# Two-layer decoder kernel: the first two products of three stages run tile by tile together

## The chip, the cores and the metric

The kernel runs on one core of a Trainium2 chip, as one program. The metric is device time in microseconds (us). TensorE (PE in the rows) does the matrix products, VectorE (DVE), ScalarE (ACT) and GpSimd (POOL) work elementwise, and all loads named here are issued from the queue of SyncE (SP). Each engine works through its own list of instructions in order and waits at semaphores for the others.

## The reference

Two layers run one after the other on 512 tokens of 1024 features. Each layer normalises its input, projects it into a mixer, adds the output product, normalises again and adds a feed-forward part.

```python
def rms_norm(x, g):
    y = xf * lax.rsqrt(jnp.mean(xf * xf, axis=-1, keepdims=True) + EPS)
    return (y * g.astype(jnp.float32)).astype(x.dtype)
...
def swiglu_ffn(h, w_gate_up, w_down):
    g, u = jnp.split(h @ w_gate_up, 2, axis=-1)
    return (jax.nn.silu(g) * u) @ w_down
...
def hybrid_layer(x, mem, positions, layer_idx, ...):
    proj = rms_norm(x, norm_mix) @ w_in
    mix, qm = dsa_mixer(proj, pos) if layer_idx % 2 == 0 else dilated_mixer(proj, pos)
    mo = memory_attention(qm, mem, norm_mem, w_mem_kv)
    x = x + jnp.concatenate([mix, mo], axis=-1) @ w_out
    return x + swiglu_ffn(rms_norm(x, norm_ffn), w_gate_up, w_down)
```

Layer 1 uses the dilated mixer: three groups of heads with strides 1, 4 and 16, each with query, key and value products and rotary angles. In both layers four more heads attend to 256 memory tokens. A last norm ends the program.

## The kernel before

Activations lie transposed in SBUF: a tile has 128 features by 512 tokens, and `xT` holds eight of them (k = 0 to 7). A product of full precision is made of three fp32r matmuls for each k: the operand is split into a high half (`xh`, `wh`) and a low half (`xl`, `wl`), and `proj` (line 228) adds `wh·xh`, `wh·xl` and `wl·xh` (lines 247 to 249) over eight tiles in one PSUM bank, so a product is 24 matmuls of 512 columns. `proj_steps` (lines 235 to 237) is the same product cut into four steps for interleaving.

A weight chunk is loaded by `load` (line 176) into one of two `wf` buffers; `wsplit` casts it to `wh` on ScalarE (line 48) and subtracts for `wl` on VectorE or GpSimd (line 51). There are three buffers each of `wh` and `wl`.

The norm is applied late. `prep` scales each tile of x by the gain into `xh` (ScalarE, line 331) and `xl` (VectorE, line 332) and sums the squares (ScalarE line 306, GpSimd line 316, VectorE line 275). `ssq_cols` turns the sum into one value per token: eight small matmuls (line 278; four in the program's order) and a chain of twelve small VectorE instructions (lines 256 to 265). `row` spreads these values into a row R: four VectorE instructions (line 288), one product with ones (line 290) and a ScalarE copy (line 293). Finished products are multiplied by R.

Three stages begin in this way; below they are called the entries. The first is `ffn(0)`, the second `layer1`, the third `ffn(1)`. At each, the last output product of the stage before still adds to `xT` tile by tile (`add_x`, line 653) while `prep` follows it, and TensorE starts the first product on the tiles as they come.

In `ffn` each step f makes two products, gate and up, from one `wf` buffer, and a gated activation (lines 676 to 679). In `layer1` the first two products are the memory heads' queries (`qm`). Then `tables` loads the angle tables from DRAM (`saved`) and multiplies them by R on GpSimd, cosine first and sine second (line 411); `memory_back` reloads the memory heads' keys and values (`kept`, line 558). Two generators are then woven: `products` (query, key and value products, `rope` on lines 376 to 384) and `attention`, which starts with `memory_attention`: scores (line 452), their maxima (line 581), exponentials (line 585), transposes (line 469) and the product with the values (line 423).

TensorE's order is the order of the code. The order on the other engines and on SyncE is set by a scheduler that simulates a timeline when the program is built. PSUM has eight banks: two named acc, three S, two T and one O; `psum_any` goes round them.

Of the kernel before, what the change touches and what calls it, by code (L numbers as in the profile page):

```python
# [19 lines left out]
NT = S // 128  # L20
MEM = 256
DFF = 2816
FT = DFF // 128
# [41 lines left out]
class _Trunk:  # L65
# [589 lines left out]
    def ffn(self, l):  # L655
        nc = self.nc
        xh, xl, parts = self.prep(2 if l == 0 else 5)
        src = self.io[f"gu{l}"]
        mh, ml = [], []
        bigs = []  # L660
        for f in range(FT):
            w = self.load(src[f], [2, 1024])
            ps = []
            for j in range(2):
                p = self.psum_any()
                self.proj(p, self.wsplit(w[:, j], nc.gpsimd if j else nc.vector), xh, xl)
                ps.append(p)
                if f == 0:
                    if j == 0:
                        cols = self.ssq_cols(parts)  # L670
                    else:
                        R = self.row(cols, NT)
            g = self.tmp("raw")
            u = self.tmp("raw")
            m = self.tmp("o")
            nc.vector.tensor_tensor(out=g, in0=ps[0], in1=R, op=ALU.mult)
            nc.scalar.activation(g, g, AF.Silu)
            nc.vector.tensor_tensor(out=u, in0=ps[1], in1=R, op=ALU.mult)  # L678
            nc.vector.tensor_tensor(out=m, in0=g, in1=u, op=ALU.mult)
            if f < 12:  # L680
                if f % 4 == 0:
                    bigs = [self.big("midh"), self.big("midl")]
                b = slice((f % 4) * 512, (f % 4 + 1) * 512)
                h, lo = bigs[0][:, b], bigs[1][:, b]
            else:
                h, lo = self.slot("mh"), self.slot("ml")
            _split2(nc, h, lo, m, nc.vector)
            mh.append(h)
            ml.append(lo)
        src = self.io[f"dn{l}"]  # L690
        for t in range(KT - 1 if l else KT):
            p = self.psum_any()
            for w, k0, k1 in self.down_weights(src[t]):
                self.down(p, w, k0, k1, mh, ml)
            self.add_x(t, p)
        if l:
            self.final(list(self.down_weights(src[KT - 1])), mh, ml)
# [264 lines left out]
    def layer1(self):  # L962
        nc, mm = self.nc, self.nc.tensor.matmul
        xh, xl, parts = self.prep(3)
        ws = self.chunks("in1", list(range(14)), lo=("gpsimd", "vector"), hi=(None, None))
        pq = []
        for j in range(2):
            p = self.psum_any()
            self.proj(p, next(ws), xh, xl)
            pq.append(p)  # L970
            if j == 0:
                cols = self.ssq_cols(parts)
            else:
                R = self.row(cols, NT)
                self.cols4 = self.ssq_cols(parts, by_residue=True)
        cs, sn = self.tables(R, 0)
        qm = [self.plain(p, R, 0.125, "qm") for p in pq]
        self.memory_back()
# [4 lines left out]
        qk0, QK = [[], []], [[[], []], [[], []]]  # L983
# [3 lines left out]
            while what not in done:  # L987
                yield

        def qk(g, dst):  # L990
            p = self.psum("acc")
            yield from self.proj_steps(p, next(ws), xh, xl)
            dst.append(self.rope(p, cs, sn, self.slot("qkh"), self.slot("qkl"), by_residue=g > 0))

        def g0_scores(pr, i):
# [111 lines left out]

        def products():
            yield from qk(0, qk0[0])
            yield from qk(0, qk0[0])  # L1110
            yield from qk(0, qk0[1])
            done.add("qk0")
            yield from qk(0, qk0[1])
            yield from values(0)
            done.add("qk1")
            done.add("v0")
            for g in range(2):
                for _ in range(2):
                    yield from qk(1, QK[0][g])
            for n, _ in enumerate(values(1)):  # L1120
                if n == 4:
                    done.add("qk2")
                yield
            yield from qk(1, QK[1][0])
            yield from qk(1, QK[1][0])
            yield from until("o0")
            yield from qk(1, QK[1][1])
            yield from qk(1, QK[1][1])
            for n, _ in enumerate(values(2)):
                if n == 0:  # L1130
                    mem_out = [(o, self.inverse(den)) for o, den in self.mem_out]
                if n == 4:
                    done.add("qk3")
                if n == 4:
                    mem_out = [self.finish_pair(*a) for a in mem_out]
                yield
            done.add("v12")
            out = self.out_proj("out1a", mem_out)
            yield from itertools.islice(out, 4)
            yield from until("all")  # L1140
            yield from out

        def attention():
# [43 lines left out]
            yield from finish(1)  # L1187
            done.add("all")

        first, second = products(), attention()  # L1190
        _weave(itertools.islice(first, 24), itertools.islice(second, 12), na=2)
        _weave(first, second)
        for _ in self.out_proj("out1b", outs):
            pass
# [182 lines left out]
```

## Time and profile before

| | |
|---|---|
| median of three runs | 1252.84 us |
| lowest and highest | 1252.38 and 1262.76 us |
| profiled execution, own time | 1258.64 us |
| its span, first to last instruction | 1256.9 us |
| mean granted TensorE clock in the span | 0.984 |

The rows used below come from the profiled execution, whose times count from the start of its span. Matmuls are pipelined, so a matmul of 512 columns is shown with 0.39 us though the next starts about 0.23 us after it. [...]

### The profile page before, as it was taken

The page shows a single profiled execution, that of the slowest core. Times are in us where ns is not written, and L with a number is a line of the kernel's source. Part 1 is how long each engine was busy: PE and PEld are TensorE (multiplying, and loading weights), DVE is VectorE, ACT ScalarE, POOL GpSimd, SP SyncE. Part 2 cuts the span into 40 slices and gives each one's busy share as a digit, 9 for nine tenths or more (in the row PEclk, how much of TensorE's full clock was granted, in tenths as well). Part 3 has the DMA queues.
Part 4 walks back from the last instruction along what each step waited for, and adds up shares of the span by engine and source line. Part 5 has one row for each costly group of instructions (what it writes and reads, how often), then busy time and mean ns, then how long its engine had stood idle before and what let it go on. Part 6 is the DMA issues. An engine that isn't in the chain of part 4 may idle for free.

```text
span 1256.9 us, 14343 instructions
## 1 busy us (share of the span) xinstructions
PE 1209.4 (96%) x5624; PEld 952.3 (76%) x5624; DVE 530.6 (42%) x1024; ACT 484.8 (39%) x852; POOL 345.6 (27%) x218
## 2 busy tenths in 40 slices
PE   9799899999999999999998999999999999999997
PEld 5368566576888888888887778887788888888886
DVE  4759823548333323322224544449433333332112
ACT  3663675424332322322222666545323222322222
POOL 0424553244212222122222223324222222211222
PEclk9889999999999999999999999999899999999999
DMA  5312212202122222222223110221122222222221
GB/s 194 123 34 101 83 37 83 69 34 101 67 101 101 101 87 82 101 64 110 107 106 116 68 68 34 67 68 67 68 101 101 98 79 92 101 93 92 92 93 67
DMA packets 29185, 108.36 MB, mean 86 GB/s; under 512 B 2494, under 2 KB 11582, under 8 KB 20670
## 3 DMA queue, kind: packets, MB, share of 16 engines
q1 hardware_dynamic: 28574, 106.93, 24.1%
q8 instruction: 44, 0.72, 0.2%
q10 hardware_dynamic: 544, 0.52, 0.1%
q14 instruction: 23, 0.19, 0.0%
HBM read 104.43 MB, written 3.01 MB: 85 GB/s over the span
## 4 chain that ended last, share of the span: by engine, by line
PE 78%; DVE 10%; DMA 4%; ACT 3%; issue 3%; POOL 1%; SPq 0%; DVEq 0%; ACTq 0%; POOLq 0%
PE psS L248 5%; PE psS L247 5%; PE psS L249 5%; PE psT L247 3%; PE psT L248 3%; PE psT L249 3%; PE psacc L247 3%; PE psacc L248 3%; PE psacc L249 3%; PE psacc L222 3%; PE psS L222 3%; PE psS L224 3%; PE psS L223 3%; PE psacc L224 3%; PE psacc L223 3%
## 5 line engine op out<-in xcount | busy, mean ns | idle before, releaser
L51 POOL TENSOR_TENSOR wl<-wf,wh 128x1024 fp32r<-128x1024 f32 x90 | 216.9, 2411 | 643.6 <-ACT wh L48 590.5
L48 ACT CAST wh<-wf 128x1024 fp32r<-128x1024 f32 (+1 forms) x163 | 167.6, 1029 | 516.5 <-issue 166.1
L51 DVE TENSOR_TENSOR wl<-wf,wh 128x1024 fp32r<-128x1024 f32 x86 | 104.0, 1210 | 88.6 <-ACT wh L48 88.6
L248 PE MATMUL psS<-xl,wh 128*128 128x512 f32 x272 | 107.7, 396 | 2.8 <-DVE xl L332 2.8
L247 PE MATMUL psS<-xh,wh 128*128 128x512 f32 x272 | 108.2, 398 | 0.0
L249 PE MATMUL psS<-xh,wl 128*128 128x512 f32 x272 | 106.9, 393 | 0.0
L247 PE MATMUL psacc<-xh,wh 128*128 128x512 f32 x192 | 76.9, 401 | 0.0
L248 PE MATMUL psacc<-xl,wh 128*128 128x512 f32 x192 | 76.9, 401 | 0.0
L249 PE MATMUL psacc<-xh,wl 128*128 128x512 f32 x192 | 76.4, 398 | 0.0
L247 PE MATMUL psT<-xh,wh 128*128 128x512 f32 x184 | 73.4, 399 | 0.0
L248 PE MATMUL psT<-xl,wh 128*128 128x512 f32 x184 | 73.3, 398 | 0.0
L249 PE MATMUL psT<-xh,wl 128*128 128x512 f32 x184 | 72.8, 396 | 0.0
L316 POOL TENSOR_TENSOR ssq<-ssq,t 128x512 f32<-128x512 f32 (+1 forms) x31 | 42.4, 1367 | 96.2 <-ACT t L306 61.0
L248 PEld LDWEIGHTS psS<-xl,wh 128*128 128x128 f32 x272 | 51.3, 188 | 14.8 <-DVE xl L332 3.3
L235 PE MATMUL psacc<-xh,wh 128*128 128x512 f32 x144 | 61.6, 428 | 0.0
L247 PEld LDWEIGHTS psS<-xh,wh 128*128 128x128 f32 x272 | 51.2, 188 | 12.3 <-issue 0.5
L249 PEld LDWEIGHTS psS<-xh,wl 128*128 128x128 f32 x272 | 51.2, 188 | 11.7
L678 DVE TENSOR_TENSOR raw<-psacc,R 128x512 f32<-128x512 f32 x22 | 15.2, 691 | 102.0 <-PE psacc L249 102.0
L237 PE MATMUL psacc<-xh,wl 128*128 128x512 f32 x144 | 56.9, 395 | 0.0
L236 PE MATMUL psacc<-xl,wh 128*128 128x512 f32 x144 | 56.8, 395 | 0.0
L653 DVE TENSOR_TENSOR xT<-xT,psacc 128x512 f32<-128x512 f32 x44 | 30.0, 683 | 39.0 <-PE psacc L224 38.8
L379 ACT COPY raw<-psacc 32x512 f32<-32x512 f32 x72 | 41.6, 578 | 6.1 <-DVE raw L376 5.1
(320 smaller groups left out, 2634.6 us busy)
## 6 DMA issues: line engine op xcount, KB each, us to landing
wf<-in_gu SPq DMA_DIRECT2D x44, 1024.0 KB
wf<-in_dn SPq DMA_DIRECT2D x16, 1024.0 KB
wf<-in_in SPq DMA_DIRECT2D x12, 1024.0 KB
wf<-in_dn SPq DMA_DIRECT2D x16, 384.0 KB
wf<-in_v SPq DMA_DIRECT2D x3, 1024.0 KB
wf<-in_in SPq DMA_DIRECT2D x5, 512.0 KB
xT<-in_x SPq DMA_DIRECT2D x8, 256.0 KB
wf<-in_mk SPq DMA_DIRECT2D x2, 1024.0 KB
```

What stands on the lines that cost most here:

```text
L48: nc.scalar.copy(hi, src)
L51: lo_engine.tensor_tensor(out=lo, in0=src, in1=hi.bitcast(F32), op=ALU.subtract)
L222: mm(out, wh[k], xh[k], start=first and k == 0, stop=False)
L223: mm(out, wh[k], xl[k], start=False, stop=False)
L224: mm(out, wl[k], xh[k], start=False, stop=last and k == n - 1)
L235: mm(out, wh[:, s], xh[k], start=k == 0, stop=False)
L236: mm(out, wh[:, s], xl[k], start=False, stop=False)
L237: mm(out, wl[:, s], xh[k], start=False, stop=k == KT - 1)
L247: mm(out, wh[:, s], xh[k], start=k == 0, stop=False)
L248: mm(out, wh[:, s], xl[k], start=False, stop=False)
L249: mm(out, wl[:, s], xh[k], start=False, stop=k == KT - 1)
L316: engine.tensor_tensor(out=parts[part], in0=parts[part], in1=sq, op=ALU.add)
```

## The change

In both feed-forward parts and in layer 1 the first two products now run together: for each tile k the three matmuls of the one and then those of the other. Their sum of squares goes to TensorE after both, one more product follows, and only then the row R. In `ffn` the gated activation of step 0 therefore comes within step 1, and the low half of step 1's gate weights moves from VectorE to GpSimd. In layer 1 the third product is the first query product of group 0, made before the row in a T bank instead of an acc bank; its rope and two further steps of `products` come ahead of the weave with the memory attention.

```diff
--- before.py
+++ after.py
@@ -658,18 +658,8 @@
         src = self.io[f"gu{l}"]
         mh, ml = [], []
         bigs = []
-        for f in range(FT):
-            w = self.load(src[f], [2, 1024])
-            ps = []
-            for j in range(2):
-                p = self.psum_any()
-                self.proj(p, self.wsplit(w[:, j], nc.gpsimd if j else nc.vector), xh, xl)
-                ps.append(p)
-                if f == 0:
-                    if j == 0:
-                        cols = self.ssq_cols(parts)
-                    else:
-                        R = self.row(cols, NT)
+
+        def swiglu(f, ps):
             g = self.tmp("raw")
             u = self.tmp("raw")
             m = self.tmp("o")
@@ -679,7 +669,7 @@
             nc.vector.tensor_tensor(out=m, in0=g, in1=u, op=ALU.mult)
             if f < 12:
                 if f % 4 == 0:
-                    bigs = [self.big("midh"), self.big("midl")]
+                    bigs[:] = [self.big("midh"), self.big("midl")]
                 b = slice((f % 4) * 512, (f % 4 + 1) * 512)
                 h, lo = bigs[0][:, b], bigs[1][:, b]
             else:
@@ -687,6 +677,22 @@
             _split2(nc, h, lo, m, nc.vector)
             mh.append(h)
             ml.append(lo)
+
+        for f in range(FT):
+            w = self.load(src[f], [2, 1024])
+            ps = [self.psum_any() for _ in range(2)]
+            ws = [self.wsplit(w[:, j], nc.gpsimd if j or f == 1 else nc.vector) for j in range(2)]
+            if f == 0:
+                self.projs(list(zip(ps, ws)), xh, xl)
+                cols = self.ssq_cols(parts)
+                first = ps
+                continue
+            for j in range(2):
+                self.proj(ps[j], ws[j], xh, xl)
+                if f == 1 and j == 0:
+                    R = self.row(cols, NT)
+                    swiglu(0, first)
+            swiglu(f, ps)
         src = self.io[f"dn{l}"]
         for t in range(KT - 1 if l else KT):
             p = self.psum_any()
@@ -963,16 +969,13 @@
         nc, mm = self.nc, self.nc.tensor.matmul
         xh, xl, parts = self.prep(3)
         ws = self.chunks("in1", list(range(14)), lo=("gpsimd", "vector"), hi=(None, None))
-        pq = []
-        for j in range(2):
-            p = self.psum_any()
-            self.proj(p, next(ws), xh, xl)
-            pq.append(p)
-            if j == 0:
-                cols = self.ssq_cols(parts)
-            else:
-                R = self.row(cols, NT)
-                self.cols4 = self.ssq_cols(parts, by_residue=True)
+        pq = [self.psum_any() for _ in range(2)]
+        self.projs([(p, next(ws)) for p in pq], xh, xl)
+        cols = self.ssq_cols(parts)
+        p = self.psum("T")
+        self.proj(p, next(ws), xh, xl)
+        R = self.row(cols, NT)
+        self.cols4 = self.ssq_cols(parts, by_residue=True)
         cs, sn = self.tables(R, 0)
         qm = [self.plain(p, R, 0.125, "qm") for p in pq]
         self.memory_back()
@@ -987,9 +990,10 @@
             while what not in done:
                 yield
 
-        def qk(g, dst):
-            p = self.psum("acc")
-            yield from self.proj_steps(p, next(ws), xh, xl)
+        def qk(g, dst, p=None):
+            if p is None:
+                p = self.psum("acc")
+                yield from self.proj_steps(p, next(ws), xh, xl)
             dst.append(self.rope(p, cs, sn, self.slot("qkh"), self.slot("qkl"), by_residue=g > 0))
 
         def g0_scores(pr, i):
@@ -1106,7 +1110,6 @@
             outs.append((hi, lo))
 
         def products():
-            yield from qk(0, qk0[0])
             yield from qk(0, qk0[0])
             yield from qk(0, qk0[1])
             done.add("qk0")
@@ -1187,8 +1190,12 @@
             yield from finish(1)
             done.add("all")
 
+        for _ in qk(0, qk0[0], p):
+            pass
         first, second = products(), attention()
-        _weave(itertools.islice(first, 24), itertools.islice(second, 12), na=2)
+        for _ in itertools.islice(first, 2):
+            pass
+        _weave(itertools.islice(first, 20), itertools.islice(second, 12), na=2)
         _weave(first, second)
         for _ in self.out_proj("out1b", outs):
             pass
```

TensorE at the entry of `ffn(0)`, end of the first product and what follows it. In these names the number counts tiles: `psS_2420` is the bank of the gate product, `psT_2471` or `psT_2421` that of the up product, `xl_2398` the second half of the low tiles. Before:

```order
L247 MATMUL psS_2420<-xh_2397,wh_2421 128x512 [waits Activation_49]
L248 MATMUL psS_2420<-xl_2398,wh_2421 128x512 [waits DVE_49]
L249 MATMUL psS_2420<-xh_2397,wl_2422 128x512
L278 MATMUL psacc_2449<-ones_71,ssq_2380 128x2 [waits DVE_49]
L278 MATMUL psacc_2449<-ones_71,ssq_2380 128x2 x3
L247 MATMUL psT_2471<-xh_2376,wh_2472 128x512 [waits PE_49]
L248 MATMUL psT_2471<-xl_2377,wh_2472 128x512
```

After:

```order
L247 MATMUL psS_2420<-xh_2397,wh_2422 128x512 [waits Activation_49]
L248 MATMUL psS_2420<-xl_2398,wh_2422 128x512 [waits DVE_49]
L249 MATMUL psS_2420<-xh_2397,wl_2423 128x512
L247 MATMUL psT_2421<-xh_2397,wh_2426 128x512
L248 MATMUL psT_2421<-xl_2398,wh_2426 128x512
L249 MATMUL psT_2421<-xh_2397,wl_2427 128x512
L278 MATMUL psacc_2478<-ones_71,ssq_2380 128x2 [waits DVE_49]
L278 MATMUL psacc_2478<-ones_71,ssq_2380 128x2 x3
L247 MATMUL psS_2502<-xh_2376,wh_2504 128x512
```

The up product now takes each tile right behind the gate product, and the small matmuls of the squares stand behind both.

VectorE at the same entry: the last low tile, the sum of squares and the begin of the chain for the norm (`rs_v`, `rs_i`, `rs_y`). Before:

```order
L51 TENSOR_TENSOR wl_2524<-wf_2520,wh_2523 128x1024 [waits DMAHW1_49,Activation_49,Pool_49]
L332 SCALAR_TENSOR_TENSOR xl_2398<-xT_79,gains_80,xh_2397 128x512 [waits Activation_49]
L275 TENSOR_TENSOR ssq_2380<-ssq_2380,ssq_2416 128x512 [waits Pool_49]
L256 TENSOR_SCALAR rs_v_2455<-psacc_2449 128x4 [waits PE_49]
L260 TENSOR_SCALAR rs_i_2457<-rs_v_2455 128x4 [waits DVE_49]
L261 TENSOR_SCALAR rs_y_2458<-rs_i_2457 128x4 [waits DVE_49]
L263 TENSOR_TENSOR rs_q_2459<-rs_y_2458 128x4 [waits DVE_49]
```

After:

```order
L332 SCALAR_TENSOR_TENSOR xl_2398<-xT_79,gains_80,xh_2397 128x512 [waits Activation_49] x2
L275 TENSOR_TENSOR ssq_2380<-ssq_2380,ssq_2416 128x512 [waits Pool_49]
L256 TENSOR_SCALAR rs_v_2484<-psacc_2478 128x4 [waits PE_49]
L260 TENSOR_SCALAR rs_i_2486<-rs_v_2484 128x4 [waits DVE_49]
L51 TENSOR_TENSOR wl_2594<-wf_2589,wh_2593 128x1024 [waits DMAHW2_49,Activation_49]
L261 TENSOR_SCALAR rs_y_2487<-rs_i_2486 128x4 [waits DVE_49]
L263 TENSOR_TENSOR rs_q_2488<-rs_y_2487 128x4 [waits DVE_49]
```

The low half of step 1's gate weights (`wl_2524`) has left the place ahead of the last `xl`, and the low half of step 2's gate weights (`wl_2594`) now stands inside the chain of the norm.

VectorE in layer 1, where the memory attention starts (`nm` is the maximum of the scores). Before, from the first maximum on:

```order
L581 TENSOR_REDUCE nm_4870<-psS_4864 128x2 [waits PE_49]
L581 TENSOR_REDUCE nm_4875<-psS_4865 128x2 [waits PE_49]
L51 TENSOR_TENSOR wl_5058<-wf_4988,wh_5057 128x1024 [waits DMAHW0_49,PE_49,Activation_49]
L581 TENSOR_REDUCE nm_4898<-psS_4892 128x2 [waits PE_49]
L581 TENSOR_REDUCE nm_4903<-psS_4893 128x2 [waits PE_49]
L376 TENSOR_TENSOR raw_4910<-psacc_4843,table_4819 128x512 [waits DMAHW2_49,Pool_49]
L498 RECIPROCAL den_4863<-den_4863 128x8 [waits Activation_49]
```

After, up to the second maximum and two rows on:

```order
L50 CAST wh_5093<-wf_5091 128x1024 [waits DMAHW1_49,PE_49]
L384 TENSOR_TENSOR raw_4876<-raw_4876,raw_4877 128x512 [waits Pool_49]
L51 TENSOR_TENSOR wl_5094<-wf_5091,wh_5093 128x1024 [waits DVE_49,PE_49]
L581 TENSOR_REDUCE nm_4924<-psS_4918 128x2 [waits PE_49]
L581 TENSOR_REDUCE nm_4929<-psS_4919 128x2 [waits PE_49]
L51 TENSOR_TENSOR qkl_4875<-raw_4876,qkh_4874 128x512 [waits Activation_49]
L376 TENSOR_TENSOR raw_4936<-psacc_4887,table_4850 128x512 [waits DMAHW2_49]
```

Ahead of the first maximum there now stand the rope's add of the first query product, which waits for GpSimd (`raw_4876`), and the split of the value weights (`wh_5093`, `wl_5094`).

## Rows read from the trace of the kernel before

**Rows 1.** the page, busy time of each engine (share of the span) and instructions.

```profile
PE 1209.4 (96%) x5624; PEld 952.3 (76%) x5624; DVE 530.6 (42%) x1024; ACT 484.8 (39%) x852; POOL 345.6 (27%) x218
```

**Rows 2.** who TensorE waited for: us in total, times, longest.

```profile
PE psS L452 <- DMA kept<-kept: 4.2, 1, 4.2
PE psO L248 <- DVE xl L332: 2.8, 1, 2.8
...
PE psacc L441 <- ACT raw L379: 1.8, 1, 1.8
```

**Rows 3.** windows: stretch, length, busy time by engine, then granted clock, DMA.

```profile
306.60:310.00 3.40, 3.40 (x10) 2.66 (x9) 3.09 (x10) 0.00 (x0) 1.67 (x1) 0.53 0.23 43
691.00:695.50 4.50, 3.89 (x14) 2.79 (x15) 1.29 (x2) 1.56 (x7) 1.27 (x1) 0.62 0.03 11
700.00:740.00 40.00, 38.22 (x238) 30.10 (x236) 18.14 (x27) 26.79 (x58) 10.42 (x7) 1.00 0.15 53
883.00:890.00 7.00, 7.00 (x22) 5.75 (x21) 4.17 (x17) 1.04 (x1) 2.35 (x1) 0.52 0.34 130
```

**Rows 4.** timeline of TensorE, first entry: start, length, instruction, [idle before <- releaser].

```profile
296.18 0.40 PE L247 MATMUL psS<-xh,wh 128*128 128x512 f32 x1
...
304.23 0.50 PE L248 MATMUL psS<-xl,wh 128*128 128x512 f32 x1 [2.84 <-DVE xl L332]
...
304.83 1.05 PE L278 MATMUL psacc<-ones,ssq 128*128 128x2 f32 x8
...
312.92 1.02 PE L290 MATMUL psacc<-raw,ones 128*128 128x512 f32 x2
...
319.38 0.40 PE L247 MATMUL psacc<-xh,wh 128*128 128x512 f32 x1
```

**Rows 5.** timeline of TensorE, third entry, first and seventy-third product matmul.

```profile
874.49 0.39 PE L247 MATMUL psO<-xh,wh 128*128 128x512 f32 x1
...
899.22 0.39 PE L247 MATMUL psT<-xh,wh 128*128 128x512 f32 x1
```

**Rows 6.** timeline of VectorE, first entry.

```profile
300.19 2.32 DVE L51 TENSOR_TENSOR wl<-wf,wh 128x1024 fp32r<-128x1024 f32 x1
302.43 1.75 DVE L332 SCALAR_TENSOR_TENSOR xl<-xT,gains,xh 128x512 fp32r<-128x512 f32 x1
...
306.12 2.17 DVE L260 TENSOR_SCALAR rs_i<-rs_v 128x4 int32<-128x4 int32 x1
...
310.31 0.87 DVE L288 TENSOR_SCALAR raw<-ident,rs_y 128x128 f32<-128x128 f32 x4
```

**Rows 7.** timeline of GpSimd, first entry.

```profile
296.27 7.36 POOL L316 TENSOR_TENSOR ssq<-ssq,t 128x512 f32<-128x512 f32 x4
305.89 2.38 POOL L51 TENSOR_TENSOR wl<-wf,wh 128x1024 fp32r<-128x1024 f32 x1 [2.26 <-PE psacc L278]
```

**Rows 8.** timeline of TensorE, second entry (layer 1).

```profile
669.96 0.40 PE L247 MATMUL psT<-xh,wh 128*128 128x512 f32 x1
...
675.48 0.95 PE L278 MATMUL psacc<-ones,ssq 128*128 128x2 f32 x8
...
684.41 0.48 PE L235 MATMUL psacc<-xh,wh 128*128 128x512 f32 x1
...
691.61 1.63 PE L452 MATMUL psS<-kept,qm 64*128 64x256 f32 x8 [4.20 <-DMA kept<-kept]
```

**Rows 9.** chain of waits in layer 1: start, length, what.

```profile
676.57 1.24 DVE wl L51
...
677.86 0.34 SPq L176
...
679.41 12.07 DMA kept<-kept
```

**Rows 10.** timelines of GpSimd and of VectorE in layer 1.

```profile
691.19 1.27 POOL L411 TENSOR_TENSOR table<-raw,R 128x512 f32<-128x512 f32 x1 [3.56 <-DMA raw<-saved]
...
693.21 1.29 DVE L581 TENSOR_REDUCE nm<-psS 128x2 f32<-128x512 f32 x2 [4.18 <-PE psS L452]
```

## The prediction

> **What bounds the kernel now.** I first read the page's busy times: TensorE is busy 96% of the span [rows 1], so only what shortens TensorE's own list, its waits or its slow stretches can change the time. Then who TensorE waited for: one wait of 4.2 us for `kept` in layer 1, waits of 2.8 us for the low tile `xl`, one of 1.8 us for an acc bank [rows 2]. Then the timeline around each entry: in `ffn(0)` TensorE stands 2.84 us for the last `xl` [rows 4], in `ffn(1)` as long by [rows 2], and in layer 1 it stands 4.20 us ahead of the first memory score [rows 8]. Last, the granted clock by windows, since waits may be followed by slow matmuls. They are: behind these three waits the clock falls to 0.53 for 3.40 us, to 0.52 for 7.00 us and to 0.62 for 4.50 us, while 40 us of ordinary work in layer 1 run at 1.00 [rows 3]. A stretch at granted clock c loses its length times 1 - c: 1.6, 3.3 and 1.7 us, 6.6 in all. So the three entries hold 2.84 + 2.84 + 4.20 = 9.9 us of waiting and 6.6 us of slow clock, 16.5 of 1257.
>
> A cross-check: 24 matmuls from 669.96 to 675.48 give 0.23 us a matmul [rows 8]. Three products are 72 of them, 16.6 us; with the small matmuls of the squares, 1.05, and the row's, 1.02 [rows 4], 18.6. TensorE took 23.2 from 296.18 to 319.38 [rows 4] and 24.7 from 874.49 to 899.22 [rows 5]: 4.6 and 6.1 too many, which is wait plus clock (2.84 + 1.6, 2.84 + 3.3).
>
> **The change, the feed-forward entries.** Nothing is computed less; matmuls, casts and loads are the same in number. What moves is when TensorE wants things.
>
> The last `xl`. Before, VectorE did step 1's `wl`, 2.32 us at 300.19, and then the last `xl`, 1.75 us from 302.43 [rows 6], while TensorE wanted it some 2.84 us sooner than 304.23. After, TensorE comes to the last tile behind 42 matmuls, at 296.18 + 42 x 0.23 = 305.8, later than 304.2 even if `xl` came no sooner, and without that `wl` it comes about 2.3 sooner. This wait goes for certain.
>
> What is late next: the sum of squares. GpSimd now gets step 1's low half between the adds that end at 303.63 before (four, 7.36 us [rows 7], so 1.84 each). It adds one op of 2.38 us [rows 7], so the last add ends at about 306; VectorE's add is taken at 0.65, as a maximum in [rows 10]. TensorE wants it behind 48 matmuls, at 307.2. Covered, with some 0.5 to 1 us to spare; if GpSimd is later than that, each us shows as a wait on the L278 matmuls.
>
> Then the row. It is wanted one product later: 307.2 + 1.05 + 5.5 = 313.8. The chain on VectorE starts at about 308.3. Before, its second instruction took 2.17 us from 306.12 [rows 6], and ended as GpSimd's `wl` of 2.38 us from 305.89 ended [rows 7]. The order has such a `wl` on GpSimd at that place again, so the chain is held till about 310.2. Then `wl_2594` stands in it, 1.24 us as in [rows 9]; the rest of the chain took 310.31 - 308.29 = 2.0 us, and the four writes of the row 0.87 [rows 6]. That is 314.3, 0.5 us behind TensorE; at the ends, the hold may be absent (no wait) or the whole chain 0.4 later (0.8). I take 0.4 of new wait at each entry. The later activation of step 0 lies beside TensorE's products, since the banks go round eight.
>
> [...]
>
> So each `ffn` gains 2.84 - 0.4 = 2.4 us, 4.9 for both.
>
> **The change, layer 1.** Here the wait is for a load, `kept`, which has nothing to do with `xl`. SyncE's queue goes in order. The chain reads: `wl` on VectorE at 676.57, 1.24 us, then an issue on SyncE at 677.86 and then `kept`, 12.07 us from 679.41 [rows 9]: a weight load that waits for a `wf` buffer stands ahead of `saved` and `kept`. That `wl` follows a cast whose buffer is free when TensorE has read the first product's `wh` for the last time: 675.4 before, but 680.4 now, since both products end together (46 instead of 24 matmuls from 669.96, and 5 us are 22 of them). So everything behind it comes 4.9 us later: `kept` is there at 679.41 + 12.07 + 4.9 = 696.4, and the sine table, multiplied from 691.19 [rows 10], starts at 696.1.
>
> TensorE comes to the first score behind two products, 11.0 us, the work that stood from 675.48 to 684.41 [rows 8], 8.9, and one more product of 24 matmuls, 5.5: at 695.4, some 0.3 later with a short wait for the row. So it waits about 0.7 for `kept` instead of 4.20: the added matmuls cover a load that came later, and most of the wait goes.
>
> A new wait follows. By the order, VectorE has a rope add ahead of the first maxima, which needs GpSimd's sine table (1.27 us [rows 10]) and a GpSimd product of the same size: 696.1 + 1.27 + 1.27 = 698.6. The add and a maximum are each taken at 0.65, half of the pair in [rows 10], and the `wl` between them is 1.24 again: the first two maxima end at 701.2, and the exponentials that free a score bank at about 702.4 (as long as the two maxima, 1.29). TensorE comes to the second score at 696.4 + 1.0 + 12 matmuls x 0.23 = about 700.4: 2 us of wait, which wasn't there. Behind it the order shows three more places where a bank is taken over quickly (a T bank, an acc bank, the product with the values); each lies between nothing and the 1.8 us of the acc bank in [rows 2], and I take 0.3, 1 and 1. Sum after: 0.7 + 2 + 0.3 + 1 + 1 = 5.0, against 4.2 + 1.8 = 6.0 before. Layer 1 gains 1 us, with bounds of 3 to either side.
>
> **The clock.** If no entry holds a long wait, the three slow stretches go, 6.6 us. The 1.8 us wait of [rows 2] lies in the 40 us at 1.00 [rows 3], so waits of 0.4 to 2 us should not bring them back. But the profiled execution took 1258.64 us, 5.8 more than the median of 1252.84, and it may be that the runs of the median lose less to the clock than the one traced. I count half, 3.3, with ends of nothing and 6.6.
>
> [...]
>
> **Sum.** Against the profiled execution: feed-forward -4.9, layer 1 -1.0, clock -6.6 in full: 1258.6 - 12.5 = 1246.1. Against the median, with half of the clock: 1252.84 - 4.9 - 1.0 - 3.3 = 1243.6, so 1244.
>
> **Rivals.**
> 1. The clock comes back in full in the median too, and layer 1 does as summed or better: 1252.84 - 12.5 = 1240, to 1237.5 when layer 1 gains 3 us more. For it: each of the three waits is followed by such a stretch, and the rest is at 1.00. Against: the median lies below the trace.
> 2. The gain of layer 1 and of its clock is eaten there: the waits at the scores, the T bank and the acc bank add up to 8 instead of 5, and no clock is gained anywhere. 1252.84 - 4.9 + 2 = 1250; with half of the clock of the feed-forward entries, 2.4, 1247.5. I price it at 1248. For it: VectorE's list has two waits on GpSimd ahead of work that TensorE wants.
> 3. Slower: VectorE stands at the rope add for the sine table, and with it the maxima and all that TensorE wants. Each us that the table is later than 696.1 is a us of TensorE. From 9 us later, 705, the change loses; if the shifted loads land as late again as `kept` takes, 12.07, the time is 1252.84 - 9.2 + 12.1 = 1256. For it: `saved` goes through the queue that the change delays. Against: [rows 9] shows that queue held by one wait only.
> 4. VectorE's chain for the row is held by GpSimd not once but twice, 2.38 us each [rows 7], in both feed-forward entries: the new wait there is 0.4 + 2.4 = 2.8 us, as long as the one removed, and the clock falls behind it as before. Then only layer 1 gains, 1.0 and half of its clock, 0.8: 1251. For it: the 2.17 us in the chain [rows 6] and one more low half on GpSimd. Against: the order puts that one ahead of the chain, not beside it.
>
> That the entries go on waiting for `xl` is excluded by 305.8 against 304.2.
>
> **How the numbers follow.** Forecast 0.43, rival 1 0.30, rival 2 0.17, rivals 3 and 4 0.05 each. About 1%, 12.5 us, is what a measurement of this kernel tells from no change: faster is below 1240.3, slower above 1265.4. Faster by that: two thirds of rival 1, 0.20, and the better quarter or so of the forecast, 0.13. Slower: 0.03, the bad end of rival 3. The range goes from the clock in full with layer 1 three us better, 1252.84 - 15.5 = 1237, to no clock and layer 1 three us worse than summed, 1252.84 - 5.9 + 3 = 1250.
>
> **What the changed profile would show.** Right: no wait of 2 us or more for `xl`; the fourth product's start 18.6 to 19.4 us behind the entry's first matmul; granted clock 1.00 in both feed-forward entries; the row's wait at L290 below 1 us; the weight load ahead of `kept` issued some 5 us later against the entry's start; a wait for `kept` under 1.5 us and a new one of about 2 at the second score. Wrong: a wait at L278 (GpSimd too late), a clock of 0.5 behind a short wait, or VectorE held at the rope add for more than 4 us. I would be wrong by much if the tail of layer 1's memory attention, which I priced by three guesses, opens gaps of more than 2 us each, or if the products made two steps earlier also shorten its end.

## The result and the profile after

The changed kernel took 1241.08 us (1237.89 to 1243.12, 4 runs) against 1252.61 (1248.98 to 1262.76, 4 runs): ratio 0.989, interval 0.984 to 0.994. A second group on another chip gave 0.988, interval 0.985 to 0.991. The forecast was 1244, the range 1237 to 1250, so the time lies inside it, nearer to rival 1 (1240) than to the forecast. The profiled execution has a span of 1236.0 us.

Who TensorE waited for, the lines that answer to [rows 2]: the two waits for `xl` and the one for `kept` are gone; the row costs 0.8 us in three waits, the acc bank 0.8 instead of 1.8. (Of the 2.8 for `raw`, 2.0 lie in layer 0.)

```profile
PE psS L452 <- ACT raw L585: 2.8, 2, 2.0
...
PE psacc L441 <- ACT raw L379: 0.8, 1, 0.8
...
PE psacc L290 <- DVE raw L288: 0.8, 3, 0.3
```

TensorE at the first entry (start, length, instruction, idle time before), beside [rows 4]: the squares follow 48 product matmuls without a wait, the row waits 0.21 us, and the fourth product starts 310.24 - 291.91 = 18.3 us behind the first matmul, where it was 23.2.

```profile
291.91 0.39 PE L247 MATMUL psS<-xh,wh 128*128 128x512 f32 x1
...
302.90 0.95 PE L278 MATMUL psacc<-ones,ssq 128*128 128x2 f32 x8
...
309.68 1.12 PE L290 MATMUL psacc<-raw,ones 128*128 128x512 f32 x2 [0.21 <-DVE raw L288]
310.24 0.79 PE L247 MATMUL psacc<-xh,wh 128*128 128x512 f32 x1
```

The third entry, beside [rows 5]: 877.90 - 858.71 = 19.2 us instead of 24.7, with one new wait of 0.56 us ahead of the second product's first matmul: its bank still held an output product, which VectorE had to add to the residual sum `xT` first.

```profile
858.71 0.40 PE L247 MATMUL psO<-xh,wh 128*128 128x512 f32 x1
...
860.12 0.47 PE L247 MATMUL psacc<-xh,wh 128*128 128x512 f32 x1 [0.56 <-DVE xT L653]
...
877.37 1.10 PE L290 MATMUL psacc<-raw,ones 128*128 128x512 f32 x2 [0.28 <-DVE raw L288]
877.90 0.79 PE L247 MATMUL psT<-xh,wh 128*128 128x512 f32 x1
```

VectorE and GpSimd at the first entry, beside [rows 6, 7]. The last two `xl` end at 298.82, and TensorE came to that tile at about 301.5. The squares are ready at 302.07 and wanted at 302.90: 0.8 us to spare. The chain's second instruction again ends with GpSimd's `wl` (304.08 + 1.65 against 303.31 + 2.40), and `wl` stands inside the chain.

```profile
294.80 4.02 DVE L332 SCALAR_TENSOR_TENSOR xl<-xT,gains,xh 128x512 fp32r<-128x512 f32 x2
301.38 0.69 DVE L275 TENSOR_TENSOR ssq<-ssq 128x512 f32<-128x512 f32 x1 [2.56 <-POOL ssq L316]
...
304.08 1.65 DVE L260 TENSOR_SCALAR rs_i<-rs_v 128x4 int32<-128x4 int32 x1
305.65 1.22 DVE L51 TENSOR_TENSOR wl<-wf,wh 128x1024 fp32r<-128x1024 f32 x1
...
308.75 0.87 DVE L288 TENSOR_SCALAR raw<-ident,rs_y 128x128 f32<-128x128 f32 x4
...
303.31 2.40 POOL L51 TENSOR_TENSOR wl<-wf,wh 128x1024 fp32r<-128x1024 f32 x1 [1.97 <-ACT wh L48]
```

Layer 1, TensorE, then SyncE's queue and GpSimd, beside [rows 8 to 10]. The value weights' load is issued 669.41 - 656.70 = 12.7 us behind the entry's first matmul, where it was 7.9, and `saved` and `kept` behind it; all the same the first score doesn't wait, and the second waits 0.83 us.

```profile
656.70 0.40 PE L247 MATMUL psT<-xh,wh 128*128 128x512 f32 x1
...
674.58 1.13 PE L290 MATMUL psacc<-raw,ones 128*128 128x512 f32 x2 [0.29 <-DVE raw L288]
675.54 1.80 PE L278 MATMUL psacc<-ones,ssq 128*128 128x2 f32 x8
...
684.52 1.13 PE L452 MATMUL psS<-kept,qm 64*128 64x256 f32 x8
...
690.09 1.13 PE L452 MATMUL psS<-kept,qm 64*128 64x256 f32 x6 [0.83 <-ACT raw L585]
...
669.41 0.34 SPq L176 DMA_DIRECT2D wf<-in_v  x1
669.80 1.11 SPq L164 DMA_DIRECT2D raw<-saved  x2
670.95 4.42 SPq L558 DMA_DIRECT2D kept<-kept  x4
...
683.34 1.30 POOL L411 TENSOR_TENSOR table<-raw,R 128x512 f32<-128x512 f32 x1 [4.21 <-DMA raw<-saved]
```

The clock in three windows (columns as in [rows 3]): both feed-forward entries run at 1.00, but layer 1 falls to 0.65 for 4.50 us behind the row, without a long wait ahead of it.

```profile
291.91:311.00 19.09, 18.88 (x85) 15.04 (x84) 12.91 (x24) 7.06 (x10) 12.23 (x8) 1.00 0.31 111
676.00:680.50 4.50, 4.50 (x14) 3.85 (x15) 3.05 (x9) 0.93 (x3) 1.29 (x1) 0.65 0.88 250
858.71:878.00 19.29, 18.45 (x84) 14.57 (x82) 12.85 (x24) 6.89 (x9) 11.65 (x7) 1.00 0.31 109
```

The two traces differ by 20.9 us, more than the medians. By stage: 4.3 us ahead of the first entry, where nothing was changed (the granted clock there is 0.97 before and 0.98 after); 4.9 and 5.5 at the feed-forward entries; 2.5 in layer 1 (204.5 to 202.0 from its entry to the next); and 4.1 in the rest of the first feed-forward part, where the clock is 1.00 in both. Behind the third entry the kernel after takes 0.5 us more. The last experiments come to that part.

### The profile page after: what moved, and what is told of

It reads as the page before. It is cut to its first block, busy times and chain, and to the rows that moved or that the text cites. A ratio compares the mean times of both kernels' runs of the same rounds, so it can differ in the third digit from the quotient of the medians.

```text
span 1236.0 us, 14342 instructions
## 1 busy us (share of the span) xinstructions
PE 1196.5 (97%) x5624; PEld 944.8 (76%) x5624; DVE 529.3 (43%) x1022; ACT 484.1 (39%) x852; POOL 350.2 (28%) x220
## 4 chain that ended last, share of the span: by engine, by line
PE 77%; DVE 10%; DMA 4%; issue 4%; ACT 3%; POOL 2%; SPq 0%; DVEq 0%; POOLq 0%; ACTq 0%
PE psS L249 5%; PE psS L247 5%; PE psS L248 5%; PE psT L249 3%; PE psT L247 3%; PE psT L248 3%; PE psacc L249 3%; PE psacc L247 3%; PE psacc L248 3%; PE psacc L222 3%; PE psacc L224 3%; PE psacc L223 3%; PE psS L222 3%; PE psS L224 3%; PE psS L223 3%
## 5 line engine op out<-in xcount | busy, mean ns | idle before, releaser
L51 POOL TENSOR_TENSOR wl<-wf,wh 128x1024 fp32r<-128x1024 f32 x92 | 222.7, 2422 | 618.9 <-ACT wh L48 567.4
L51 DVE TENSOR_TENSOR wl<-wf,wh 128x1024 fp32r<-128x1024 f32 (+1 forms) x84 | 99.4, 1184 | 80.0 <-ACT wh L48 80.0
L247 PE MATMUL psacc<-xh,wh 128*128 128x512 f32 x192 | 75.5, 393 | 0.6 <-DVE xT L653 0.6
L249 PE MATMUL psT<-xh,wl 128*128 128x512 f32 x192 | 75.5, 393 | 0.0
L249 PE MATMUL psacc<-xh,wl 128*128 128x512 f32 x192 | 75.5, 393 | 0.0
L248 PE MATMUL psacc<-xl,wh 128*128 128x512 f32 x192 | 74.9, 390 | 0.0
L235 PE MATMUL psacc<-xh,wh 128*128 128x512 f32 x136 | 58.1, 428 | 0.0
L237 PE MATMUL psacc<-xh,wl 128*128 128x512 f32 x136 | 54.1, 398 | 0.0
L236 PE MATMUL psacc<-xl,wh 128*128 128x512 f32 x136 | 54.0, 397 | 0.0
L247 PEld LDWEIGHTS psacc<-xh,wh 128*128 128x128 f32 x192 | 36.1, 188 | 8.7 <-issue 1.2
```

Source lines behind the costliest of these rows:

```text
L51: lo_engine.tensor_tensor(out=lo, in0=src, in1=hi.bitcast(F32), op=ALU.subtract)
L235: mm(out, wh[:, s], xh[k], start=k == 0, stop=False)
L236: mm(out, wh[:, s], xl[k], start=False, stop=False)
L237: mm(out, wl[:, s], xh[k], start=False, stop=k == KT - 1)
L247: mm(out, wh[:, s], xh[k], start=k == 0, stop=False)
L248: mm(out, wh[:, s], xl[k], start=False, stop=False)
```

## The experiments

"Entry" is the time from an entry's first product matmul to its fourth product, "layer 1" the time from its entry to that of `ffn(1)`.

**The parts alone.** `e1_ffn_only` is the changed kernel with layer 1 as before; `e2_layer1_only` the kernel before with the changed layer 1.

> Only the two feed-forward entries are changed, layer 1 is as before. Theory (the entries' waits and the slow clock behind them are the gain): from an entry's first product matmul to its fourth product 18.3 and 19.2 us, as in the changed kernel, against 23.2 and 24.7 before, so about 10.4 us less than before, ratio 0.992; layer 1 stays at 204.5 us with its 4.2 us wait for kept and a clock near 0.6 behind it. Rival (the gain of the change comes mostly from layer 1 or from outside the three stages): under 4 us, ratio 0.997 or more.

Measured: ratio 0.992, interval 0.989 to 0.995, with entries of 18.3 and 19.2 us and the 4.35 us wait for `kept` in layer 1. As the theory had it.

> Only layer 1 is changed, both feed-forward parts are as before. Theory: layer 1 takes 202 us instead of 204.5, the feed-forward entries keep 23.2 and 24.7 us; about 2.5 us less than before, ratio 0.998, not to be told from no change. Rival (layer 1 carries half of the gain or more): 6 us less or more, ratio 0.995.

Measured: ratio 0.999, interval 0.996 to 1.002; layer 1 203.5 us, the feed-forward entries 23.2 and 23.1 us (at the third the slow stretch was shorter here than in the trace of before). The waits at the first two scores are 0.93 and 1.29 us. The feed-forward entries carry the gain. What layer 1 gives depends on the clock: it took 202.0 to 203.7 us in the six traces with the changed layer 1 and 204.4 to 207.3 in the four that have it as before (the kernel before, `e1_ffn_only`, `e4_low_half_moved_alone`, `e6_filled_wait`).

**Which move of the feed-forward entry counts.** `e3_low_half_on_vector` is the changed kernel with

```diff
-            ws = [self.wsplit(w[:, j], nc.gpsimd if j or f == 1 else nc.vector) for j in range(2)]
+            ws = [self.wsplit(w[:, j], nc.gpsimd if j else nc.vector) for j in range(2)]
```

> The changed kernel, but the low half of step 1's gate weights stays on VectorE, ahead of the last xl, as before the change. Theory (the pairing alone covers xl: TensorE comes to the last tile behind 42 matmuls instead of 21): no wait for xl over 0.3 us, entries of 18.3 and 19.2 us to within 0.3, the time of the changed kernel. Rival (the move to GpSimd is part of the gain): a wait for the last xl of 0.5 us or more at L248 in both feed-forward entries, and with a lower clock behind it 2 us more in each.

Measured: 1238.2 us, ratio 0.986, interval 0.982 to 0.991; no wait for `xl`, entries of 18.3 and 19.2 us. Beside the pairing the move to GpSimd shows no gain. `e4_low_half_moved_alone` is the kernel before with that move only:

```diff
-                self.proj(p, self.wsplit(w[:, j], nc.gpsimd if j else nc.vector), xh, xl)
+                self.proj(p, self.wsplit(w[:, j], nc.gpsimd if j or f == 1 else nc.vector), xh, xl)
```

> The kernel before with one edit: the low half of step 1's gate weights is made on GpSimd. Theory (without the pairing the sum of squares is late next, since GpSimd has 2.4 us more to do ahead of it): the wait for xl falls from 2.84 to 0.6 us or less, a wait of about 4 us comes up at the squares' matmuls, L278, and the entries stay at 23 and 24.5 us, the time of before within 3 us. Rival (the wait for xl was the bound and goes with that edit): entries of 20 to 21 us, 6 to 8 us less in all, ratio 0.995 or less.

Measured: 0.6% slower, ratio 1.006, interval 1.003 to 1.008, entries of 27.2 and 28.4 us. The wait for `xl` fell only to 1.70 us, and the squares came 4.6 us late in both parts: the theory's place, with a price above the theory's. VectorE's rows at that entry show why: with GpSimd's `wl` from 299.48 to 302.30 beside them the two last `xl` take 3.96 us, where they took 1.18 and 1.75 in the kernel before beside GpSimd's adds, and the last add of the squares takes 2.81 instead of 0.68 beside the next `wl`, 0.55 us of it behind that one's end. One line of the waits, two of VectorE, one of GpSimd:

```profile
PE psacc L278 <- DVE ssq L275: 9.2, 2, 4.6
```
```profile
298.88 3.96 DVE L332 SCALAR_TENSOR_TENSOR xl<-xT,gains,xh 128x512 fp32r<-128x512 f32 x2
305.35 2.81 DVE L275 TENSOR_TENSOR ssq<-ssq 128x512 f32<-128x512 f32 x1 [2.51 <-POOL ssq L316]
...
305.27 2.34 POOL L51 TENSOR_TENSOR wl<-wf,wh 128x1024 fp32r<-128x1024 f32 x1
```

So the low half on GpSimd costs something where no pairing covers it, 0.6% here.

`e5_row_at_once` makes the row ahead of the third product:

```diff
-                cols = self.ssq_cols(parts)
+                R = self.row(self.ssq_cols(parts), NT)
                 first = ps
...
-                    R = self.row(cols, NT)
                     swiglu(0, first)
```

> The changed kernel, but in the feed-forward parts the row R is made right behind the squares, ahead of the third product instead of behind it. Theory (the third product covers the chain on VectorE): TensorE waits 5 to 6 us at the row, L290, in each feed-forward entry, its clock falls behind it, entries of 24 to 26 us, 11 to 15 us more than the changed kernel: about the time of before. Rival (the pairing alone is the gain, the row's later place is worth nothing): a wait under 2 us and under 4 us more in all.

Measured: ratio 1.001 to before, interval 0.999 to 1.004; entries of 27.0 and 27.5 us, longer than the theory's 24 to 26, with waits of 5.76 and 5.85 us at the row. Pairing without the later row gives everything back.

```profile
PE psacc L290 <- DVE raw L288: 11.9, 3, 5.9
```

**The clock.** `e6_filled_wait` is the kernel before with work of no use in place of the wait:

```diff
+            if k == KT - 1:
+                for i in range(12):
+                    mm(spare, wh[:, s], xh[i % 4], start=True, stop=True)
```

> The kernel before, with 12 matmuls of no use put ahead of the last tile of the first product in both feed-forward parts (into the second product's bank, which is overwritten later): TensorE works through the 2.8 us in which it waited for xl. Theory (the wait itself brings the clock down and costs more than its own length): granted clock 1.00 in both entries, entries of 21.4 us each although as much time passes ahead of xl, 1.7 and 3.3 us less than before; and the slower pitch of matmuls (0.233 instead of 0.229 us, for the 250 us of the gate and up products) that stands behind some of these drops in the traces so far does not come up; 5 us less than before or up to 10 with the pitch, ratio 0.992 to 0.996. Rival (the clock's fall and the slower pitch come by themselves, not from the wait): the clock falls in at least one entry, or the pitch of 0.233 shows without a fall ahead of it; the time of before.

Measured: ratio 0.996, interval 0.994 to 0.999, 4.2 us less by the medians, a little under the theory's 5. The useful work behind the wait starts no sooner than before, but the clock stays up: entries of 21.35 and 21.42 us at 1.00, instead of 23.2 and 24.7 (the columns are length, busy time by engine, granted clock, DMA).

```profile
294.69:316.04 21.35, 21.23 (x94) 16.64 (x93) 17.32 (x29) 9.06 (x12) 9.63 (x6) 1.00 0.28 99
869.63:891.05 21.42, 21.30 (x95) 16.63 (x93) 17.31 (x29) 9.06 (x12) 9.62 (x6) 1.00 0.28 99
```

**Layer 1's loads.** `e9_kept_first` is the kernel before with one line moved; `e10_ffn_and_kept_first` has the changed feed-forward parts too, and `e12_ffn_and_kept_first_again` is the same kernel beside the changed one, `e11_changed_again`. `e13_kept_and_angles_first` is the changed kernel with `kept` and the angle tables loaded first.

```diff
+        self.memory_back()
         xh, xl, parts = self.prep(3)
...
-        self.memory_back()
```

> The kernel before with one edit: the four loads of kept are issued at the begin of layer 1, ahead of the value weights' load; the order on the compute engines is the same. Theory (the 4.2 us wait is the place of the loads in SyncE's queue, nothing else): kept is there before the first score, no wait of more than 0.5 us there, and no slow clock behind it: 4.2 + 1.7 = 5.9 us off layer 1, to about 198.6 us. Rival (the wait only changes its name, to the angle tables that still come behind the value weights, or to VectorE): a new wait of 2 us or more within 15 us behind the first score, layer 1 at 202 us or more.

Measured: no wait at either score and no fall of the clock in layer 1, which took 198.8 us, as the theory had it; every compute engine did the same instructions in the same order. The times, ratio 0.998 with an interval from 0.995 to 1.001, can't show it. SyncE issues `kept` six us ahead of the entry at 664.83:

```profile
658.63 1.76 SPq L558 DMA_DIRECT2D kept<-kept  x4
663.15 0.38 SPq L176 DMA_DIRECT2D wf<-in_in  x1
672.73 0.33 SPq L176 DMA_DIRECT2D wf<-in_v  x1
```

> The feed-forward entries as changed, layer 1 as before but with the loads of kept issued first. Theory: the gains add up, 10.4 + 5.9 = 16 us below before, ratio 0.987, some 3 us below the changed kernel. Rival (the new wait of layer 1 takes the place of the old): as the changed kernel or 2 us above it, ratio 0.990 to 0.992.

Measured: 1239.2 us, ratio 0.989, interval 0.984 to 0.993; layer 1 198.6 us.

> The changed kernel itself, without an edit, on the chip of the next two, for a direct comparison. Expected by every theory: ratio to before between 0.984 and 0.992, entries of 18.3 and 19.2 us, the pitch of matmuls at 0.229 us in both feed-forward parts since no wait of 2 us stands ahead of them.

Measured: 1241.7 us, ratio 0.988, interval 0.985 to 0.991; the same entries. Here the clock did not fall behind layer 1's row, and the waits at the scores are 1.08 and 1.25 us. It fell later, to 0.69 and 0.85, behind a wait of 1.85 us for an acc bank that stands in the kernel before as well:

```profile
PE psacc L1046 <- ACT raw L379: 1.9, 1, 1.9
...
PE psS L452 <- ACT raw L585: 1.2, 1, 1.2
PE psS L452 <- DMA kept<-kept: 1.1, 1, 1.1
```
```profile
809.00:813.00 4.00, 2.88 (x7) 2.43 (x8) 0.41 (x1) 1.53 (x3) 4.00 (x3) 0.69 0.00 0
813.00:816.00 3.00, 3.00 (x12) 2.79 (x12) 0.69 (x1) 0.21 (x1) 0.41 (x1) 0.85 0.02 5
```

> The feed-forward entries as changed, layer 1 as before with the loads of kept issued first: the same kernel as above, beside the changed kernel on one chip. Theory (by the spans of layer 1, 198.6 against 202.0 to 203.5): 3 to 5 us below the changed kernel. Rival (the times of both are the same and the difference of the spans is chance of the clock): within 2 us.

Measured: 1236.7 us, ratio 0.986, interval 0.983 to 0.989: 4.9 us below the changed kernel by the medians. The two intervals overlap, so the runs alone don't settle it; layer 1 does, 198.6 and 200.2 us in the two traces of this kernel against 202.0 to 203.7 in the six of the changed layer 1. It has the lowest median of the versions tried. The longer of its two traces has the fall of the clock behind the wait of 1.8 us for an acc bank that the prediction took for harmless [rows 2, 3]:

```profile
713.18 0.39 PE L441 MATMUL psacc<-wh,xh 128*128 128x256 f32 x1 [1.79 <-ACT raw L379]
```
```profile
712.50:717.50 5.00, 4.32 (x23) 4.32 (x24) 1.38 (x2) 1.71 (x4) 1.51 (x2) 0.66 0.00 0
```

> The changed kernel with the loads of kept and of the angle tables issued at the begin of layer 1. Theory (the waits at the first two scores, 0.9 and 1.3 us in the runs of the changed layer 1 in which the clock doesn't fall ahead of them, both come from loads that stand behind the value weights' load: kept itself, and the sine table that VectorE's rope add waits for): both under 0.3 us, layer 1 about 2 us shorter, 201 to 201.5 us. Rival (VectorE's order, not the loads): the wait at the second score stays at 1 us or more, layer 1 at 202.5 us or more.

Measured: 1239.9 us, ratio 0.988, interval 0.985 to 0.991. Both waits at the scores are gone, as the theory had it, and layer 1 took 202.3 us, not 201 to 201.5: the clock fell in two places, behind the row (0.57 over 4.00 us) and behind the acc bank's wait (0.66 over 5.00 us), where `e11_changed_again` had one fall. By these figures each fall cost about 1.7 us (an estimate, length times one minus clock); without them the estimate is 198.9 us, about what layer 1 as before takes with `kept` moved (198.6 in `e10_ffn_and_kept_first`, where the clock doesn't fall). So the theory of the loads holds, and layer 1 missed its forecast by the clock.

**A second pitch of TensorE.** The same 200 us of gate and up products, at clock 1.00, hold 859 matmuls in the trace of before and 875 or 876 in others (windows of the kernel before, then two of `e9_kept_first`, then the changed kernel). That is 0.233 against 0.229 us a matmul, some 4.6 us over the 250 us of these products (from its entry to that of layer 1 the first feed-forward part takes 373.8 us in the trace of before and 369.2 in that of `e9_kept_first`, with entries of 23.2 us in both), and so the 4.1 us that no edit explains.

```profile
330.00:530.00 200.00, 200.00 (x859) 162.01 (x858) 68.58 (x90) 58.51 (x72) 43.33 (x18) 1.00 0.27 95
```
```profile
330.00:530.00 200.00, 200.00 (x875) 164.11 (x874) 69.31 (x91) 60.02 (x74) 44.57 (x19) 1.00 0.27 95
900.00:1100.00 200.00, 200.00 (x859) 162.01 (x858) 68.49 (x90) 58.29 (x72) 43.25 (x18) 1.00 0.27 95
```
```profile
330.00:530.00 200.00, 200.00 (x876) 164.09 (x875) 69.14 (x91) 58.66 (x72) 43.33 (x18) 1.00 0.26 92
```

It showed in three of the six feed-forward parts traced with the entry of before (one each of the kernel before, `e2_layer1_only` and `e9_kept_first`), in the trace of before from 314.0 to about 557 us, setting in behind the row's product, 4.1 us after the clock had returned at 309.9; in none of the four of `e4_low_half_moved_alone` and `e5_row_at_once`, where the clock falls too; and in none of the sixteen traced without a fall of the clock at the entry (`e6_filled_wait` among them). The theory that each return of the clock draws the pitch anew was put to a test with eight stalls:

```diff
+                if j == 0 and f in (5, 9, 13, 17):
+                    self.stall(ps[0], R)
```

> The changed kernel with one stall of TensorE in each of steps 5, 9, 13 and 17 of both feed-forward parts: a matmul of no use waits for nine multiplications by R in a chain on VectorE, some 7 us. Theory (the pitch of the fp32r matmuls is set anew at each return of the clock, to 0.229 or to 0.233 us, and stays so until the next disturbance): the clock falls behind each stall, and of the eight stretches of some 40 us behind them at least one and at most six run at 0.233, each with one pitch all through. Rival (the pitch has nothing to do with stalls or the clock's return): all eight run alike, at the pitch of the stretch ahead of the first stall. 70 to 110 us longer than the changed kernel.

Measured: eight waits of 9.0 us, the clock down behind each, 1341 us, and the pitch at 0.229 us behind all eight. The theory of a draw at each return falls, or its chance is far below the three in six of the first entries. What sets the slower pitch stays open.

```profile
PE psacc L291 <- DVE raw L289: 72.1, 8, 9.0
```

## Why the prediction came out as it did

**The feed-forward entries: right, and for the reasons given.** The fourth product at 18.3 and 19.2 us lies in the forecast window of 18.6 to 19.4, but for 0.3. The wait for `xl` went by the pairing (`e3_low_half_on_vector`: 42 matmuls of cover instead of 21). The squares had 0.8 us to spare where 0.5 to 1 was expected, and `e4_low_half_moved_alone` shows them late, at L278, as soon as that cover is missing. The row cost 0.21 and 0.28 us, where 0.4 was taken, and `e5_row_at_once` shows what the third product hides. Rival 4, a second hold of the chain, didn't come up. Not foreseen: the 0.56 us for `xT` in the third entry.

**Layer 1's waits: right.** The issue shifted by 4.8 us (4.9 worked out). Three traces have no clock fall in layer 1: `e14_eight_stalls` with the changed layer 1 (202.0 us), and `e9_kept_first` and `e10_ffn_and_kept_first` with that of before but for the wait for `kept` (198.8 and 198.6 us). The time from each instruction of TensorE to the next, summed by line, gives what lies between `e14_eight_stalls` and `e10_ffn_and_kept_first`: 1.1 us for `kept` (0.7 worked out), 2.0 at the scores (2.0; 1.27 of it is the listed wait, the rest stands between the matmuls of that score), 0.5 at the transposes (0.3), 0.6 at the product with the values (1), 0.3 for the row, and 1.1 less at the acc bank, which now costs 0.8 (1). So the waits are 1.1 + 2.0 + 0.5 + 0.8 + 0.6 = 5.0, as the sum had them. In four more traces (`e2_layer1_only`, `e3_low_half_on_vector`, `e5_row_at_once`, `e11_changed_again`) the listed waits are 0.9 to 1.2 for `kept` and 1.25 to 1.3 at the second score, and layer 1 is 0.8 to 1.1 us shorter than in the trace of before, with one fall of the clock in each of the five; the sum said 1.0 for the waits alone. In the trace of the changed kernel the slow clock behind the row delayed TensorE by some 1.6 us (4.50 us at 0.65), more than it waits for `kept` in these, so no such wait is left in it. Rivals 2 and 3 didn't happen: the waits stayed below what they replaced, and the sine table came 5.4 us later, not 9.

**The clock: the term of the sum that was mis-sized.** Half was counted, 3.3 us. In the two feed-forward entries all of it came back: 1.00 in every trace of the changed entries, and `e6_filled_wait` shows that there the wait causes the fall, 1.9 and 3.3 us of entry beyond its own length. In layer 1 it did not come back: the fall only moved, behind the row or behind the acc bank's 1.85 us, and of the six traces `e14_eight_stalls` alone had none. So a clock of 0.5 behind a short wait, one of the prediction's own signs of being wrong, did come there (0.50 from 678.00 to 680.50 in the trace of the changed kernel, behind the row's wait of 0.29 us), and what causes the fall behind the row, in one of the six and in `e13_kept_and_angles_first`, was not tested. The sentence that waits of up to 2 us don't bring the clock down was wrong: it rested on one trace, and in `e12_ffn_and_kept_first_again` the clock fell behind the very wait that it named. The half was taken because the median lay below the trace, not from a mechanism: more came back at the entries and nothing in layer 1, so that the sum still came near is in part luck. Taken over whole runs, span times one minus mean clock is an estimate of what the clock costs: its median is 21.3 us over 62 runs of before and 13.6 over 9 of the changed kernel, 7.7 less, part of it ahead of the first entry, where nothing changed. Rival 1 had the clock back in full, 6.6 us in the three entries; in the feed-forward entries that came, in layer 1 it didn't.

**The waits at a clock of 1.00, and the rest.** With the wait filled and the clock at 1.00 the feed-forward entries of before took 21.35 and 21.42 us (`e6_filled_wait`); the changed ones take 18.32 and 19.20, so 3.0 and 2.2 us are won there, 5.2 where 4.9 was forecast. Layer 1 of before without a fall of the clock would take 198.6 + 4.2 = 202.8 us (an estimate from `e10_ffn_and_kept_first` and the wait for `kept`), the changed one took 202.0: 0.8 us where 1.0 was forecast. That is 6.0 us of waits against the forecast's 5.9, and 5.2 us of clock in the two feed-forward entries (in the trace of before) against its 3.3: 11.2 us together, beside 11.5 by the medians of the first comparison.

Over whole runs, span times mean clock, an estimate of the time at a clock of 1.00, has a median of 1232.1 us before (62 runs) and 1225.4 after (9 runs), 6.7 less. The mean clock is given to three places, so each of these values is uncertain by 0.6 us. Before, 38 of them lie from 1227.5 to 1233.7, around 1231.6, 23 from 1234.3 to 1238.0, around 1235.8, and one at 1241.3; the nine after lie between 1224.9 and 1226.4. The spacing of the two groups, 4.2 us, is near that of one slow feed-forward part, 4.6 us, and the trace of before, which has one, belongs to the second. That the slower pitch makes the groups is argued from this and not shown; the gap between them is narrow. Against the first group the change is worth 1231.6 - 1225.4 = 6.2 us of waits, which agrees with the 6.0 above.

## What to carry to other kernels

When an operand comes tile by tile, let two products share the tiles: the wait is covered by work that must be done anyway, and what else is late (here the squares and the row) should be moved by one product as well, or the gain goes there. Count a wait on a tensor engine with the slow clock behind it, measured by filling the wait with idle matmuls; here it was 1.9 and 3.3 us on 2.8 in one trace, and 1.7 for the second of them in another. A load that is late only because its issue stands behind a load that waits for a buffer is mended in the queue: moving the loads of `kept` ahead gave layer 1 more (198.6 to 200.2 us) than the reordering of its products (202.0 to 203.7).

## What the runs showed of the hardware

TensorE ran the same fp32r products at two pitches under a granted clock of 1.00: 859 and 875 matmuls in 200 us, 0.233 and 0.229 us each. In the trace of before it kept the slower from 314.0 to about 557 us.

The granted clock fell in some places, to 0.50 in the traces of before and of the changed kernel. In the latter it read 0.50 from 678.00 to 680.50 us, and a matmul of 512 columns started every 0.43 us there instead of every 0.23. It fell behind the waits of 2.8 us for `xl` in all six (0.53 over 3.40 us and 0.52 over 7.00 in the trace of before); behind a stretch with only a 0.28 or 0.29 us wait, one row product and eight matmuls of two columns in two of the seven traces that have this stretch (0.65 over 4.50 us in the changed kernel's, 0.57 over 4.00 in that of `e13_kept_and_angles_first`); behind the wait of 1.8 us of [rows 2] for an acc bank in one of the seven traces that have it (0.66 over 5.00 us in that of `e12_ffn_and_kept_first_again`); and behind a later wait of 1.8 to 1.9 us for an acc bank in six of the fourteen traces (0.69 over 4.00 us in that of `e11_changed_again`).

A 128x4 integer VectorE instruction (line 260) took 0.16 or 0.17 us with GpSimd idle. It took 1.43 to 2.19 us in the five places of the traces of before and after where GpSimd was in a 128x1024 subtraction, and each time it ended 0.02 to 0.03 us behind GpSimd's instruction (at the first entry of before 306.12 + 2.17 against 305.89 + 2.38). In `e4_low_half_moved_alone` a 128x512 add took 2.81 us beside such a subtraction; in the kernel before it took 0.68 with GpSimd idle.
